# An attention, recurrence and feed-forward block on one core: wider products for the recurrence, modulation moved later, softmax steps of two heads together

## The chip, the cores and the metric

The kernel runs on one core of a Trainium2 chip. The metric is the device time of one execution in microseconds. Of the kernel before there are three timed runs (median 1793.35 us, 1793.25 to 1795.22) and one more execution that was profiled (1793.77 us).

## The reference, cut to what matters

One block is computed for 256 tokens of 2048 features in 32-bit floats (T = 256, D = 2048).

```python
mod = silu(c) @ ada_w + ada_b                 # 6 x 2048: sh1, sc1, g1, sh2, sc2, g2
h = rmsnorm(x) * norm1_g * (1 + sc1) + sh1
z = h @ w_in                                  # q, 6 x kv, gates, lx, ly, ga, gb
o_a = attention(...)                          # compressed, selected and window branch, gated
u = causal_dwconv(lx)                         # 4 taps
r, i = sigmoid(u @ w_a + b_a), sigmoid(u @ w_i + b_i)     # 16 blocks of 128
a = exp(8 * r * log_sigmoid(lam)); b = sqrt(1 - a*a) * i * u
o_b = gelu(ly) * scan(a, b)
merged = sigmoid(ga) * (o_a @ proj_a) + sigmoid(gb) * (o_b @ proj_b)
x = x + g1 * (merged @ w_out)
h = rmsnorm(x) * norm2_g * (1 + sc2) + sh2
x = x + g2 * conv_glu_ffn(h); out = rmsnorm(x) * final_g
```

## The kernel before

**Products in three parts.** Every large product is taken with weights and activations split in a high and a low part. A weight piece of 1 MB is loaded by SyncE's queue into one of four buffers (`stage`, L97 to L100). For each half of it ScalarE copies the high part (L107) and VectorE subtracts it from the weights for the low part (L108), into one of three pairs of `hi` and `lo` buffers (`split`). TensorE adds high by high, high by low and low by high into PSUM. An activation tile `h1[:, kt]` holds its high part in columns 0 to 255 and its low part in columns 256 to 511.

There are three forms of this in the kernel. `dense_tok` (L192) has tokens on the partitions and multiplies 512 columns of weights at a time. `dense_pair` (L114) has features on the partitions: the high weights are multiplied by all 512 columns of the activation tile in one instruction, the low weights by the first 256 columns. Its result lies in two banks of PSUM, one for each of two blocks of 128 features, as two halves of 256 columns that are still to be added. The feed-forward adds them with one VectorE reduction (`reduce`, L225). `dense_pair1` (L172) is used by the recurrence's 16 products (L715, L765): three instructions of 256 columns for each tile (L185, L187, L188), 96 in a call, both blocks of features in a single bank, and nothing to add. One ScalarE instruction of 512 columns takes the result away: a copy into `lx` (L716), or the Gelu (L767). Banks for all these products come from one pool of four (L112).

**Modulation.** `mod` has 96 pieces of 1 MB, one for each 128 of its 12288 columns. The first 32 are needed at the start. The other 64 wait in a list (L513), in the order g1, sc2, sh2, g2. `filler(n)` takes n of them: each loads a piece through the same four buffers and queue as the weights, VectorE multiplies it by the activated condition and sums it (L234), and adds the bias (L235). Before, fillers stand behind the recurrence's products (two behind each of the eight calls that make `lx`, L720, and four in all at L773), behind the merge's projections (L797, 28 in all) and in the first half of the feed-forward (16).

**Order of the work.** A scheduling pass of the compiler orders the instructions of each engine from the program order, with estimated times. `tc.high_priority(200)` moves some earlier. `tc.keep_in_program_order` keeps the instructions so marked in the order of the program: all loads, and the products of `dense_pair`. Engines run their queues in order.

**The stages around the change.** Attention (L632 to L703) handles four heads of one group and 128 tokens in a unit, eight units in all. For each head: scores (L667, L670), the maximum (L676, L677), the exponential with its sum (L679), a reciprocal and the gate (L681 to L683), the scaling (L686), transposes through one PSUM bank (L689) and copies out of it (L691). The eight calls for `lx` are issued among the units. Then come four steps of the recurrence (L725 to L773): convolution, gate products, sigmoids, exponentials and square roots, the scan, and two calls for the Gelu branch each. The merge follows (L781 to L809: gates and projections, `dense_tok`), then the output projection (L839 to L855), whose rows become the input of the feed-forward. Columns 256 and 257 of the tiles `hp` hold the shift sh2 (L823 to L826); the first product of the feed-forward (`dense_shift`, L148 to L150) reads them.

Of the kernel before, what the change touches and what calls it, by code (L numbers as in the profile page):

```python
# [38 lines left out]
def block_kernel(tc, x_t, x_n, gf_row, cols_d, consts_d, ada_w, w_kv0, w_kv, w_v, w_gate, w_q, cmp_w, cmp_w2,  # L39
# [16 lines left out]
    with ExitStack() as es:  # L56
# [57 lines left out]
        def dense_pair(pieces, rhs):  # L114
# [4 lines left out]
            for ip, ap in enumerate(pieces):  # L119
                raw = stage(ap)  # L120
                for half in range(2):
                    hl = split(raw, half * 1024, 1024)
                    done = [0, 0]
                    for w in (0, 0, 1, 0, 1, 0, 1, 1) + (0, 1) * 4 if ip + half == 0 else (0, 1) * 8:
                        f, k = done[w] // 4, done[w] % 4
                        done[w] += 1
                        kt = ip * 8 + half * 4 + k
                        r = rhs(kt)
                        tc.keep_in_program_order(
                            PE.matmul(ps[f][:, 0:256] if w else ps[f], hl[w][:, k * 256 + f * 128:k * 256 + f * 128 + 128],  # L130
                                      r[:, 0:256] if w else r, start=(kt == 0 and not w), stop=(kt == n - 1 and w == 1),
                                      skip_group_check=True))
            return ps

# [37 lines left out]
        def dense_pair1(pieces, rhs):  # L172
            p = bank()
            n = len(pieces) * 8
            for ip, ap in enumerate(pieces):
                raw = stage(ap)
                for half in range(2):
                    hi, lo = split(raw, half * 1024, 1024)
                    for f in range(2):
                        o = p[:, f * 256:f * 256 + 256]  # L180
                        for k in range(4):
                            kt = ip * 8 + half * 4 + k
                            sl = slice(k * 256 + f * 128, k * 256 + f * 128 + 128)
                            r = rhs(kt)
                            PE.matmul(o, hi[:, sl], r[:, 0:256], start=(kt == 0 and f == 0), stop=False,  # L185
                                      skip_group_check=True)
                            PE.matmul(o, hi[:, sl], r[:, 256:512], start=False, stop=False, skip_group_check=True)  # L187
                            PE.matmul(o, lo[:, sl], r[:, 0:256], start=False, stop=(kt == n - 1),  # L188
                                      skip_group_check=True)
            return p  # L190

        def dense_tok(pieces, lhs, late=None):  # L192
# [15 lines left out]
            for ip, ap in enumerate(pieces):  # L208
                raw = stage(ap)
                hold = late is not None and ip >= len(pieces) - 2  # L210
                for half in range(2):
# [6 lines left out]
                    for j in range(2):  # L218
                        products(j, k0, *hl)
            for j in range(2 if held else 0):  # L220
# [411 lines left out]
        def attention(g, t):  # L632
# [31 lines left out]
            nj = 2 * (t + 1)  # L664
            for hh in range(4):
# [9 lines left out]
                sm = tmp.tile([128, 6], F32, tag="sm", bufs=2, name="sm")  # L675
                V.tensor_reduce(sm[:, 0:2], s[:, 0:2 * nk].rearrange("p (b n) -> p b n", b=2), axis=AX, op=ALU.max)  # L676
                V.tensor_scalar(sm[:, 0:2], sm[:, 0:2], -SCALE, None, op0=ALU.mult)  # L677
                for b in range(2):
                    A.activation(p[:, b * nk:b * nk + nk], s[:, b * nk:b * nk + nk], AF.Exp, bias=sm[:, b:b + 1],  # L679
                                 scale=SCALE, accum_out=sm[:, 2 + b:3 + b])  # L680
                V.tensor_scalar(sm[:, 2:4], sm[:, 2:4], 1e-30, None, op0=ALU.max)  # L681
                V.reciprocal(sm[:, 2:4], sm[:, 2:4])
                V.tensor_tensor(sm[:, 4:6], sm[:, 2:4], gates[:, hh, 1:3], op=ALU.mult)  # L683
                for b in range(2):
                    pb = p[:, b * nk:b * nk + nk]
                    V.tensor_scalar(pb, pb, sm[:, 4 + b:5 + b], None, op0=ALU.mult)  # L686
                tp = psx.tile([128, 512], F32, tag="t", bufs=1, name="tp")
                for j in range(nj):
                    PE.transpose(tp[:, j * 128:j * 128 + 128], p[:, j * 128:j * 128 + 128], ident)  # L689
                for n in range(t + 1):  # L690
                    A.activation(pT[n][:, :, hh, :], tp[:, n * 256:n * 256 + 256].rearrange("p (j q) -> p j q", q=128),  # L691
                                 AF.Copy)
# [21 lines left out]
        for pr in range(8):  # L714
            pl = dense_pair1([w_lru[pr, k] for k in range(2)], h1r)  # L715
            A.activation(lx[pr // 2][:, 2 * (pr % 2):2 * (pr % 2) + 2],  # L716
                         pl.rearrange("p (f t) -> p f t", f=2), AF.Copy)
            if units:
                attention(*units.pop(0))
            filler(2)  # L720
# [4 lines left out]
        for bt in range(4):  # L725
# [37 lines left out]
            for h in range(2):  # L763
                pr = bt * 2 + h
                pl = dense_pair1([w_lru[8 + pr, k] for k in range(2)], h1r)  # L765
                gl = u[:, 2 * h:2 * h + 2]
                tbl(A.activation(gl, pl.rearrange("p (f t) -> p f t", f=2), AF.Gelu_apprx_tanh))  # L767
# [5 lines left out]
                filler(2 if pr % 4 == 0 else 0)  # L773
# [7 lines left out]
        for n in range(4):  # L781
            m = []
            for s, rhs in ((0, lambda kt: oA[:, kt]), (1, lambda kt: oB[kt // 2][:, kt % 2])):
# [3 lines left out]
                else:  # L787
                    ps = dense_tok([w_gates[n - 1, s, k] for k in range(4)], h1r)
# [231 lines left out]
```

## Time and profile before

| | |
|---|---|
| median of three timed runs | 1793.35 us |
| profiled execution | 1793.77 us |
| its span, first to last instruction | 1792.0 us |
| TensorE busy | 1771.6 us (99%) |
| VectorE busy | 1350.5 us (75%) |
| ScalarE busy | 881.9 us (49%) |
| mean granted TensorE clock | 0.997 |
| read from HBM | 425.72 MB, 239 GB/s over the span |

The span leaves 1.8 us of the profiled execution outside it. Matmuls overlap in the record, since the next one starts before the last one's modelled end. What a matmul costs in a stream is therefore the distance from one start to the next, not the duration in its row.

### The profile page before, as it was taken

The page shows a single profiled execution, that of the slowest core. Times are in us where ns is not written, and L with a number is a line of the kernel's source. Part 1 is how long each engine was busy: PE and PEld are TensorE (multiplying, and loading weights), DVE is VectorE, ACT ScalarE, POOL GpSimd, SP SyncE. Part 2 cuts the span into 40 slices and gives each one's busy share as a digit, 9 for nine tenths or more (in the row PEclk, how much of TensorE's full clock was granted, in tenths as well). Part 3 has the DMA queues.
Part 4 walks back from the last instruction along what each step waited for, and adds up shares of the span by engine and source line. Part 5 has one row for each costly group of instructions (what it writes and reads, how often), then busy time and mean ns, then how long its engine had stood idle before and what let it go on. Part 6 is the DMA issues. An engine that isn't in the chain of part 4 may idle for free.

```text
span 1792.0 us, 25746 instructions
## 1 busy us (share of the span) xinstructions
PE 1771.6 (99%) x10262; PEld 1545.9 (86%) x10262; DVE 1350.5 (75%) x1976; ACT 881.9 (49%) x1202; POOL 0.2 (0%) x4
## 2 busy tenths in 40 slices
PE   8999999999999999999999999999999999999997
PEld 7999898888999888888888998888888888888886
DVE  7998897998698766767765997888555677766555
ACT  5644464655578444444445644444433444444443
POOL 0000000000000000000000000000000000000000
PEclk9999999999999999999999999999999999999999
DMA  9999864665646867777775566777655555555552
GB/s 350 379 335 355 288 245 161 235 212 203 221 173 227 303 237 290 286 292 281 294 266 195 186 235 235 282 282 282 239 193 200 191 188 188 188 188 188 190 198 106
DMA packets 64200, 429.50 MB, mean 240 GB/s; under 512 B 7088, under 2 KB 7376, under 8 KB 15568
## 3 DMA queue, kind: packets, MB, share of 16 engines
q1 hardware_dynamic: 63792, 427.08, 66.2%
q8 instruction: 80, 1.31, 0.3%
q10 hardware_dynamic: 288, 0.79, 0.1%
q14 instruction: 40, 0.33, 0.1%
HBM read 425.72 MB, written 2.11 MB: 239 GB/s over the span
## 4 chain that ended last, share of the span: by engine, by line
PE 86%; DVE 6%; DMA 4%; issue 2%; ACT 2%; SPq 0%; DVEq 0%; ACTq 0%
PE P L130 26%; PE P L204 12%; PE P L205 12%; PE P L203 12%; PE P L187 3%; PE P L188 3%; PE P L185 3%; DMA raw<-ada_w 2%; DVE lo L108 2%; PE P L464 2%; PE P L466 2%; PE P L465 2%; PE P L149 1%; PE P L148 1%; PE P L150 1%
## 5 line engine op out<-in xcount | busy, mean ns | idle before, releaser
L107 ACT ACTIVATE hi<-raw 128x1024 fp32r<-128x1024 f32 x588 | 622.0, 1060 | 764.5 <-PE P L205 325.5
L108 DVE TENSOR_TENSOR lo<-raw,hi 128x1024 fp32r<-128x1024 f32 x588 | 717.1, 1222 | 370.5 <-ACT hi L107 369.7
L130 PE MATMUL P<-h,hi 128*128 128x512 f32 x1344 | 463.9, 394 | 0.0
L130 PE MATMUL P<-h,lo 128*128 128x256 f32 x1344 | 366.4, 278 | 0.0
L130 PEld LDWEIGHTS P<-h,hi 128*128 128x128 f32 x1344 | 249.1, 188 | 54.9
L130 PEld LDWEIGHTS P<-h,lo 128*128 128x128 f32 x1344 | 252.4, 188 | 4.2
L234 DVE SCALAR_TENSOR_TENSOR raw<-raw,crow 128x2048 f32<-128x2048 f32 x64 | 146.2, 2285 | 3.6 <-DMA raw<-ada_w 3.2
L188 PE MATMUL P<-h,lo 128*128 128x256 f32 x512 | 147.6, 289 | 0.8 <-DVE lo L108 0.8
L187 PE MATMUL P<-h,hi 128*128 128x256 f32 x512 | 146.7, 287 | 0.0
L185 PE MATMUL P<-h,hi 128*128 128x256 f32 x512 | 146.7, 287 | 0.0
L464 PE MATMUL P<-h,hi 128*128 128x256 f32 x384 | 107.9, 285 | 0.3 <-ACT hi L107 0.3
L465 PE MATMUL P<-h,hi 128*128 128x256 f32 x384 | 107.6, 284 | 0.0
L466 PE MATMUL P<-h,lo 128*128 128x256 f32 x384 | 102.2, 284 | 0.0
L188 PEld LDWEIGHTS P<-h,lo 128*128 128x128 f32 x512 | 97.8, 191 | 1.8 <-DVE lo L108 1.4
L187 PEld LDWEIGHTS P<-h,hi 128*128 128x128 f32 x512 | 97.9, 191 | 1.4 <-issue 1.2
L185 PEld LDWEIGHTS P<-h,hi 128*128 128x128 f32 x512 | 97.9, 191 | 1.0 <-issue 0.7
L204 PE MATMUL P<-lo,ua 128*128 128x512 f32 x240 | 93.5, 390 | 0.3 <-DVE lo L108 0.3
L205 PE MATMUL P<-hi,ua 128*128 128x512 f32 x240 | 93.4, 389 | 0.0
L203 PE MATMUL P<-hi,ua 128*128 128x512 f32 x240 | 83.6, 389 | 0.0
L204 PE MATMUL P<-lo,h 128*128 128x512 f32 x192 | 75.5, 393 | 0.0
L464 PEld LDWEIGHTS P<-h,hi 128*128 128x128 f32 x384 | 74.0, 193 | 1.1 <-ACT hi L107 0.5
L205 PE MATMUL P<-hi,h 128*128 128x512 f32 x192 | 74.9, 390 | 0.0
(281 smaller groups left out, 3131.6 us busy)
## 6 DMA issues: line engine op xcount, KB each, us to landing
raw<-ada_w SPq DMA_DIRECT2D x96, 1024.0 KB, 5.0
raw<-w_up SPq DMA_DIRECT2D x96, 1024.0 KB, 4.8
raw<-w_down SPq DMA_DIRECT2D x48, 1024.0 KB, 4.9
raw<-w_lru SPq DMA_DIRECT2D x32, 1024.0 KB, 4.9
raw<-w_proj SPq DMA_DIRECT2D x32, 1024.0 KB, 5.1
raw<-w_gates SPq DMA_DIRECT2D x24, 1024.0 KB, 6.5
raw<-w_out SPq DMA_DIRECT2D x16, 1024.0 KB, 4.9
raw<-w_kv SPq DMA_DIRECT2D x24, 512.0 KB, 6.7
```

Of the source, the lines that this page charges most:

```text
L107: A.activation(hi[:, :n], raw[:, lo_col:lo_col + n], AF.Copy)
L108: V.tensor_tensor(lo[:, :n], raw[:, lo_col:lo_col + n], hi[:, :n].bitcast(F32), op=ALU.subtract)
L130: PE.matmul(ps[f][:, 0:256] if w else ps[f], hl[w][:, k * 256 + f * 128:k * 256 + f * 128 + 128], r[:, 0:256] if w else r, start=(kt == 0 ...
L185: PE.matmul(o, hi[:, sl], r[:, 0:256], start=(kt == 0 and f == 0), stop=False, skip_group_check=True)
L187: PE.matmul(o, hi[:, sl], r[:, 256:512], start=False, stop=False, skip_group_check=True)
L188: PE.matmul(o, lo[:, sl], r[:, 0:256], start=False, stop=(kt == n - 1), skip_group_check=True)
L203: PE.matmul(ps[j], xh, hi[:, w], start=(kt == 0), stop=False, skip_group_check=True)
L204: PE.matmul(ps[j], xh, lo[:, w], start=False, stop=False, skip_group_check=True)
L205: PE.matmul(ps[j], xl, hi[:, w], start=False, stop=(kt == n - 1), skip_group_check=True)
L234: V.scalar_tensor_tensor(raw, raw, 1.0, row, op0=ALU.mult, op1=ALU.mult, accum_out=modc[:, c:c + 1])
L464: PE.matmul(o, hi[:, sl], h1[:, kt, 0:256], start=first and f % 2 == 0, stop=False, skip_group_check=True)
L465: PE.matmul(o, hi[:, sl], h1[:, kt, 256:512], start=False, stop=False, skip_group_check=True)
```

## The change

`dense_pair1` goes; the recurrence's 16 products are made by `dense_pair`, whose new argument leaves the order of its instructions to the scheduling pass. A new helper adds the two halves: ScalarE copies the second half to its destination, and VectorE adds the first half to it. Gelu then reads the sum from SBUF. Of the modulation pieces, 4 instead of 16 stand in the loop over `lx` and none instead of 4 in the recurrence; 36 instead of 28 are in the merge, placed between the weight pieces of one product, and 8 in the output projection. The 16 in the feed-forward stay. The shift columns of `hp` are written behind the output projection. In attention two heads share the steps from the clamp to the gate, and their scaling, transposes and copies follow behind both heads' exponentials.

```diff
-        def dense_pair(pieces, rhs):
+        def dense_pair(pieces, rhs, pinned=True):
 
 
...
-                    for w in (0, 0, 1, 0, 1, 0, 1, 1) + (0, 1) * 4 if ip + half == 0 else (0, 1) * 8:
+                    for w in (0, 0, 1, 0, 1, 0, 1, 1) + (0, 1) * 4 if pinned and ip + half == 0 else (0, 1) * 8:
...
-                        tc.keep_in_program_order(
-                            PE.matmul(ps[f][:, 0:256] if w else ps[f], hl[w][:, k * 256 + f * 128:k * 256 + f * 128 + 128],
-                                      r[:, 0:256] if w else r, start=(kt == 0 and not w), stop=(kt == n - 1 and w == 1),
-                                      skip_group_check=True))
+                        mm = PE.matmul(ps[f][:, 0:256] if w else ps[f],
+                                       hl[w][:, k * 256 + f * 128:k * 256 + f * 128 + 128], r[:, 0:256] if w else r,
+                                       start=(kt == 0 and not w), stop=(kt == n - 1 and w == 1), skip_group_check=True)
+                        if pinned:
+                            tc.keep_in_program_order(mm)
             return ps
+
+        def add_halves(dst, p):
+            A.activation(dst, p[:, 256:512], AF.Copy)
+            with tc.high_priority(200):
+                V.tensor_tensor(dst, p[:, 0:256], dst, op=ALU.add)
 
...
-        def dense_tok(pieces, lhs, late=None):
+        def dense_tok(pieces, lhs, late=None, fills=()):
...
+                if ip in fills:
+                    filler()
...
+            sm = tmp.tile([128, 2, 4, 2], F32, tag="sm", bufs=2, name="sm")
+            heads = []
+
+            def turn_heads(hh):
+                p = heads[hh]
+                for b in range(2):
+                    pb = p[:, b * nk:b * nk + nk]
+                    V.tensor_scalar(pb, pb, sm[:, 1, hh, b:b + 1], None, op0=ALU.mult)
+                tp = psx.tile([128, 512], F32, tag="t", bufs=1, name="tp")
+                for j in range(nj):
+                    PE.transpose(tp[:, j * 128:j * 128 + 128], p[:, j * 128:j * 128 + 128], ident)
+                for n in range(t + 1):
+                    A.activation(pT[n][:, :, hh, :], tp[:, n * 256:n * 256 + 256].rearrange("p (j q) -> p j q", q=128),
+                                 AF.Copy)
+
             for hh in range(4):
...
-                V.tensor_scalar(sm[:, 2:4], sm[:, 2:4], 1e-30, None, op0=ALU.max)
-                V.reciprocal(sm[:, 2:4], sm[:, 2:4])
-                V.tensor_tensor(sm[:, 4:6], sm[:, 2:4], gates[:, hh, 1:3], op=ALU.mult)
...
+                heads.append(p)
+                if hh % 2 == 0:
+                    continue
+                w = sm[:, 1, hh - 1:hh + 1]
+                V.tensor_scalar(w, w, 1e-30, None, op0=ALU.max)
+                V.reciprocal(w, w)
+                V.tensor_tensor(w, w, gates[:, hh - 1:hh + 1, 1:3], op=ALU.mult)
+                turn_heads(hh - 1)
+                turn_heads(hh)
...
         for pr in range(8):
-            pl = dense_pair1([w_lru[pr, k] for k in range(2)], h1r)
-            A.activation(lx[pr // 2][:, 2 * (pr % 2):2 * (pr % 2) + 2],
-                         pl.rearrange("p (f t) -> p f t", f=2), AF.Copy)
+            ps = dense_pair([w_lru[pr, k] for k in range(2)], h1r, False)
+            for f in range(2):
+                add_halves(lx[pr // 2][:, 2 * (pr % 2) + f], ps[f])
             if units:
                 attention(*units.pop(0))
-            filler(2)
+            filler(pr % 2)
...
-                pl = dense_pair1([w_lru[8 + pr, k] for k in range(2)], h1r)
+                ps = dense_pair([w_lru[8 + pr, k] for k in range(2)], h1r, False)
                 gl = u[:, 2 * h:2 * h + 2]
-                tbl(A.activation(gl, pl.rearrange("p (f t) -> p f t", f=2), AF.Gelu_apprx_tanh))
+                for f in range(2):
+                    add_halves(gl[:, f], ps[f])
+                tbl(A.activation(gl, gl, AF.Gelu_apprx_tanh))
...
-                filler(2 if pr % 4 == 0 else 0)
...
-                    ps = dense_tok([w_gates[n - 1, s, k] for k in range(4)], h1r)
+                    ps = dense_tok([w_gates[n - 1, s, k] for k in range(4)], h1r, fills=(1, 3))
...
-                ps = dense_tok([w_proj[n, s, k] for k in range(4)], rhs)
+                ps = dense_tok([w_proj[n, s, k] for k in range(4)], rhs, fills=(0, 1, 3))
...
-                filler(2 if n == 0 else 4)
...
-        filler(max(0, len(fill) - 16))
+        assert len(fill) == 24
...
-        for n in range(8):
-            sh = modc[:, 48 + 2 * n:50 + 2 * n].unsqueeze(2).to_broadcast([128, 2, 2])
-            A.activation(hp[n][:, :, 0, 256:258], sh, AF.Copy)
-            V.tensor_tensor(hp[n][:, :, 1, 256:258], sh, hp[n][:, :, 0, 256:258].bitcast(F32), op=ALU.subtract)
-
...
-            ps = dense_tok([w_out[n, k] for k in range(4)], lambda kt: mg[kt // 2][:, kt % 2])
+            ps = dense_tok([w_out[n, k] for k in range(4)], lambda kt: mg[kt // 2][:, kt % 2],
+                           fills=(0, 1, 3) if n < 2 else (0, 2) if n == 2 else ())
...
+        for n in range(8):
+            sh = modc[:, 48 + 2 * n:50 + 2 * n].unsqueeze(2).to_broadcast([128, 2, 2])
+            A.activation(hp[n][:, :, 0, 256:258], sh, AF.Copy)
+            V.tensor_tensor(hp[n][:, :, 1, 256:258], sh, hp[n][:, :, 0, 256:258].bitcast(F32), op=ALU.subtract)
```

## Rows read from the trace of the kernel before

**Rows 1.** The page's first part: span, busy time and instructions of each engine.
```profile
span 1792.0 us, 25746 instructions
...
PE 1771.6 (99%) x10262; PEld 1545.9 (86%) x10262; DVE 1350.5 (75%) x1976; ACT 881.9 (49%) x1202; POOL 0.2 (0%) x4
```

**Rows 2.** The page's chain that ended last, shares by engine.
```profile
PE 86%; DVE 6%; DMA 4%; issue 2%; ACT 2%; SPq 0%; DVEq 0%; ACTq 0%
```

**Rows 3.** Stretches: length, PE, PEld, DVE, ACT, POOL busy, clock, DMA share, GB/s.
```profile
285.00:585.00 300.00, 298.68 (x2166) 267.68 (x2165) 258.56 (x579) 195.12 (x378) 0.00 (x0) 1.00 0.57 204
480.00:585.00 105.00, 104.18 (x823) 102.18 (x822) 91.07 (x130) 83.07 (x110) 0.00 (x0) 1.00 0.58 209
585.00:985.00 400.00, 400.00 (x1796) 330.63 (x1795) 272.80 (x309) 177.67 (x210) 0.00 (x0) 1.00 0.75 272
660.00:680.00 20.00, 20.00 (x89) 16.33 (x88) 16.26 (x18) 8.08 (x8) 0.00 (x0) 1.00 0.99 384
1060.00:1240.00 180.00, 180.00 (x1038) 157.27 (x1037) 157.98 (x226) 80.09 (x91) 0.00 (x0) 1.00 0.74 265
```

**Rows 4.** TensorE's waits from 285 to 585 us: total, times, longest.
```profile
PEld P L188 <- DVE lo L108: 1.4, 3, 0.9
PE P L188 <- DVE lo L108: 0.8, 2, 0.7
```

**Rows 5.** Timeline of TensorE in a recurrence product: start, duration; 27 starts apart.
```profile
483.74 0.28 PE L188 MATMUL P<-h,lo 128*128 128x256 f32 x1
...
486.98 0.28 PE L188 MATMUL P<-h,lo 128*128 128x256 f32 x1
```

**Rows 6.** The chain in order of time, second half's feed-forward products: start, length.
```profile
1385.19 266.87 PE P L130 x1536
```

**Rows 7.** Timeline of TensorE behind an attention unit's small products.
```profile
427.25 0.36 PE L188 MATMUL P<-h,lo 128*128 128x256 f32 x1
427.45 0.28 PE L185 MATMUL P<-h,hi 128*128 128x256 f32 x1
```

**Rows 8.** Groups by line, ACT and DVE: count, busy us, mean ns, idle before.
```profile
L808 ACT ACTIVATE mg<-turn 128x256 fp32r<-128x256 f32 x16 | 5.2, 377 | 2.8 <-PE turn L806 2.8
L809 DVE TENSOR_TENSOR mg<-turn,mg 128x256 fp32r<-128x256 f32 x16 | 6.0, 415 | 0.0
L716 ACT ACTIVATE lx<-P 128x512 f32<-128x512 f32 x8 | 4.6, 579 | 0.0
L767 ACT ACTIVATE lt<-P 128x512 f32<-128x512 f32 x8 | 4.7, 589 | 0.0
L892 ACT ACTIVATE fgl<-ct 128x512 f32<-128x512 f32 x24 | 15.1, 628 | 5.1 <-DVE ct L889 5.0
L234 DVE SCALAR_TENSOR_TENSOR raw<-raw,crow 128x2048 f32<-128x2048 f32 x64 | 146.2, 2285 | 3.6 <-DMA raw<-ada_w 3.2
L235 DVE TENSOR_TENSOR modc<-modc,cols 128x1 f32<-128x1 f32 x64 | 9.7, 151 | 0.0
L681 DVE TENSOR_SCALAR sm<-sm 128x2 f32<-128x2 f32 x32 | 5.2, 162 | 3.3 <-ACT p L679 3.2
L682 DVE RECIPROCAL sm<-sm 128x2 f32<-128x2 f32 x32 | 5.1, 160 | 0.3
L683 DVE TENSOR_TENSOR sm<-sm,gsig 128x2 f32<-128x2 f32 x32 | 5.0, 155 | 0.3
```

**Rows 9.** Timelines of DVE, PE and ACT around the recurrence's third step.
```profile
543.42 1.22 DVE L758 TENSOR_TENSOR lt<-lt 128x1024 f32<-128x1024 f32 x1
...
546.02 0.28 PE L187 MATMUL P<-h,hi 128*128 128x256 f32 x1
...
551.73 0.60 ACT L767 ACTIVATE lt<-P 128x512 f32<-128x512 f32 x1
```

**Rows 10.** Timelines of PE and ACT where the feed-forward begins.
```profile
983.97 0.28 PE L148 MATMUL P<-hp,hi 128*128 128x258 f32 x1
...
986.75 0.18 ACT L837 ACTIVATION_READ_ACCUMULATOR junk<-res 128x1 f32 x1
```

More of the change, by code (lines that the diff above doesn't have):

```diff
@@ L170, in up @@
             return take
[L172 to L190, printed above, removed]
-        def dense_tok(pieces, lhs, late=None):
+        def dense_tok(pieces, lhs, late=None, fills=()):
             ps = [bank(), bank()]
@@ L674, in attention @@
                     p = tmp.tile([128, 512], F32, tag=("r", "iu", "tt")[hh - 1], bufs=1, name="p")
-                sm = tmp.tile([128, 6], F32, tag="sm", bufs=2, name="sm")
-                V.tensor_reduce(sm[:, 0:2], s[:, 0:2 * nk].rearrange("p (b n) -> p b n", b=2), axis=AX, op=ALU.max)
-                V.tensor_scalar(sm[:, 0:2], sm[:, 0:2], -SCALE, None, op0=ALU.mult)
+                V.tensor_reduce(sm[:, 0, hh], s[:, 0:2 * nk].rearrange("p (b n) -> p b n", b=2), axis=AX, op=ALU.max)
+                V.tensor_scalar(sm[:, 0, hh], sm[:, 0, hh], -SCALE, None, op0=ALU.mult)
                 for b in range(2):
-                    A.activation(p[:, b * nk:b * nk + nk], s[:, b * nk:b * nk + nk], AF.Exp, bias=sm[:, b:b + 1],
-                                 scale=SCALE, accum_out=sm[:, 2 + b:3 + b])
-                V.tensor_scalar(sm[:, 2:4], sm[:, 2:4], 1e-30, None, op0=ALU.max)
-                V.reciprocal(sm[:, 2:4], sm[:, 2:4])
-                V.tensor_tensor(sm[:, 4:6], sm[:, 2:4], gates[:, hh, 1:3], op=ALU.mult)
[L684 to L692, printed above, removed]
+                    A.activation(p[:, b * nk:b * nk + nk], s[:, b * nk:b * nk + nk], AF.Exp, bias=sm[:, 0, hh, b:b + 1],
+                                 scale=SCALE, accum_out=sm[:, 1, hh, b:b + 1])
+                heads.append(p)
[7 more added lines that the diff above has]
+                turn_heads(hh)
             PE.matmul(oT, vcmp[:, g * 128:g * 128 + 128], pcT[0:47], start=True, stop=False,
```

## The prediction

> **What bounds the kernel now.** I read the page's first part first: TensorE is busy for 1771.6 of 1792.0 us [rows 1]. The chain of waits agrees, with 86% on TensorE [rows 2]. A busy record can hide waits, so I then took stretches. From 285 to 585 us, where attention and the recurrence lie, TensorE is idle for 300.00 - 298.68 = 1.3 us; from 585 to 985 us, merge and output projection, it is not idle at all [rows 3]. Its waits in the first stretch are for VectorE's low halves, 1.4 and 0.8 us at most, partly the same time [rows 4]. So the time is the sum of what TensorE issues, and an edit on another engine counts only where it makes TensorE wait. The granted clock is 1.00, the upper level of 2.4 GHz, in every stretch [rows 3].
>
> **The products.** In a recurrence product 27 instructions of 256 columns start within 486.98 - 483.74 = 3.24 us, 0.120 us each [rows 5]; one tile costs three, 0.360 us. The new form already runs in the feed-forward: 1536 instructions, half of them 512 and half 256 columns wide, take 266.87 us [rows 6], so a tile costs 266.87 / 768 = 0.3475 us. Sixteen calls have 32 tiles each: 512 x (0.360 - 0.3475) = **6.4 us less**. TensorE streams the same 768 columns for a tile; only one instruction's fixed part goes. As 256 columns at 2.4 GHz last 0.1067 us, that part is 13.3 ns in rows 5, and 512 x 13.3 ns is 6.8 us, near the same.
>
> The Trainium skill ("TensorE: Matmul & The Clock Gate", Back-to-back issue gap) puts the fixed part of an isolated warm matmul at about 2.5 ns. By it the products would give 512 x 2.5 ns = 1.3 us, an estimate from that page. The trace does not agree, since rows 5 leave 13.3 ns.
>
> The order of the new calls is not fixed as in rows 6; the scheduling pass may group them otherwise. The columns and instructions are the same, so I cost this at nothing; if it placed a low product ahead of its low half, TensorE would wait as in rows 4, some 0.7 us at a time.
>
> **Adding the halves** brings 32 ScalarE copies and 32 VectorE additions of 256 columns from PSUM. The nearest rows have 0.377 and 0.415 us [rows 8]: 12.1 us of ScalarE and 13.3 us of VectorE. Eight copies of 0.579 us go (4.6 us); eight Gelus read SBUF, 0.628 instead of 0.589 us (0.3 us more) [rows 8]. None of this lies on TensorE. It could hold its banks: a call now takes two of the four, not one, so a call's halves must be taken away before the next call but one begins, one call or 32 x 0.3475 = 11.1 us later. In the third step the first call's last product starts about 546.0 us and its Gelu runs at 551.73 us [rows 9], six microseconds later, which would still be in time. The new copy is free earlier: it writes where L758 reads, and L758 is over at 543.42 + 1.22 = 544.6 us, before the products end [rows 9]. Cost: nothing.
>
> **The modulation.** Sixteen pieces leave the stretch 285 to 585 us. Each is 2.285 + 0.151 = 2.44 us of VectorE [rows 8], 39 us in all. With the three small softmax steps done for two heads at once (16 x (0.162 + 0.160 + 0.155) = 7.6 us less [rows 8]), VectorE goes from 258.6 to 258.6 - 39 - 7.6 + 13.3 = 225 us of 300 and ScalarE from 195.1 to 195.1 + 7.8 = 203 us [rows 3]. What TensorE can win there is its whole idle time, 1.3 us, or nothing; I take half, **0.7 us**.
>
> The 16 pieces go to merge and output projection, and their 16 loads of 1.05 MB pass SyncE's queue in front of loads of gate, projection and output weights and of the rows of x. VectorE there goes from 272.8 to 312 us of 400, 78% [rows 3]; in the feed-forward TensorE stays fully busy with VectorE at 157.98 / 180 = 88% [rows 3]. The DMA goes from 272 x 400 = 109 MB to 126 MB, 314 GB/s. From 660 to 680 us 384 GB/s moved while TensorE did not stop [rows 3]. The tightest place is the first output product: four weight pieces, three modulation pieces, the g1 row (1 MB) and half a megabyte of x, 8.5 x 1.05 = 8.9 MB within about 96 x 20 / 89 = 21.6 us, where 384 GB/s need 23.2 us. The four buffers ahead may cover the 1.6 us or not: 0 to 1.6 us.
>
> **The shift columns** now come behind the output projection. Their last modulation piece stands in its third product, so the fourth (21.6 us) hides them if the pass puts them there. If they queue behind the last squares, which end at 986.75 + 0.18 us, TensorE, which begins the feed-forward at 983.97 us [rows 10], waits some 3 us. I take 0.7 us for this and the DMA together, nearer the lower ends, since both have a cover of 20 us or of four buffers.
>
> **Two heads at once** leave TensorE's instructions in attention as they are. Going back from small products to large ones costs 427.45 - 427.25 - 0.12 = 0.08 us [rows 7]. If the transposes of two heads ran together, half of 32 such returns would go, 1.3 us; as they share one PSUM bank, the second head's must wait for copies, so I take nothing. The first head's transposes wait for the second's exponential, with the dense products as cover; the 1.3 us of idle time in the stretch says how well they cover today. A loss is held by the same rows at a few tenths of a microsecond for a head.
>
> **Sum.** 6.4 + 0.7 - 0.7 = 6.4 us less than the profiled execution's 1793.77 us: 1787.4 us. The median of the timed runs stands 0.4 us lower, so I predict **1787.0 us**, 0.35% less. With both upper bounds and no loss it is 6.4 + 1.3 + 1.3 = 9.0 us, 1784.3 us from the median.
>
> **Rivals.**
>
> First, **the recurrence's queues take the place of the wait.** From 480 to 585 us ScalarE is busy for 83.1 us and VectorE for 91.1 us of 105 [rows 3]. The recurrence has only four modulation pieces in its program to lose, and the change adds 16 copies, 16 additions and 0.3 us of Gelu: 6.0 + 6.6 + 0.3 = 12.9 us in two queues that run in order. If each delays a split that TensorE waits for, and it decides as soon as the three pairs of `hi` and `lo` run dry, the kernel takes 1793.35 - 6.4 + 12.9 = **1799.9 us**, slower. For it speaks that both engines would be near 88% of a shorter stretch and that rows 4 show this wait already. Against it: VectorE gets some of its 39 us back just before, so it enters the recurrence ahead, and TensorE idles only 0.8 us there today. Chance 0.08.
>
> Second, **part of the gain is eaten** in that way, or by the shift columns and the DMA (3 + 1.6 us, together 1791.5 us), or by half of the 12.9 us (1793.4 us). Chance 0.12.
>
> Third, **the wider instruction saves nothing**, because time goes by columns: 768 columns at 0.120 / 256 us are 0.360 us again, 1793.35 us. Rows 6 speak against it; it needs the new calls to run worse than the same form in the feed-forward. By the 2.5 ns of the Trainium skill's page named above it would be 1793.35 - 1.3 = 1792.1 us, an estimate and much the same case. Chance 0.04.
>
> Fourth, the waits of the stretch hide more than the idle time shows, and the time falls below 1784.3 us. Chance 0.04. The forecast keeps 0.72.
>
> **Numbers.** A measurement of this kernel can tell about 0.2%, 3.6 us, from no change. Below 1789.8 us lie the forecast and the fourth rival, 0.76; the second and third are within 0.2%, 0.16; the first is slower, 0.08. The range 1784.3 to 1793.4 us holds the forecast and most of the second and third, about 8 in 10.
>
> **What would show it.** Right: the recurrence's calls show 64 instructions, 0.3475 us for a pair, and TensorE's idle time from attention to the recurrence's end stays near 1 us; the same stage is about 6 us shorter and all later stages have their old lengths. Wrong: waits of TensorE for low or high halves of some microseconds in the recurrence, a wait for a bank or for `hp` at the start of the feed-forward, a wait for a modulation piece ahead of VectorE in the output projection, or pairs that cost 0.36 us.

## The result and the profile after

The changed kernel is slower: a median of 1808.6 us (1806.53 to 1809.74, four runs) against 1793.3 us of the kernel before, ratio 1.0083 with a 95% interval of 1.0067 to 1.0099. The profiled execution took 1807.54 us. The page's first part and its chain, by engine:

```profile
span 1805.7 us, 24688 instructions
...
PE 1773.0 (98%) x9750; PEld 1520.2 (84%) x9750; DVE 1359.6 (75%) x1960; ACT 890.6 (49%) x1228; POOL 0.2 (0%) x4
...
PE 76%; DMA 11%; DVE 7%; ACT 2%; issue 2%; DVEq 0%; ACTq 0%
```

The 512 matmuls are gone (10262 to 9750, [rows 1]), yet TensorE's busy time is no shorter and the span is 13.7 us longer. The chain has 11% on DMA, where it had 4% [rows 2]. The same columns as in [rows 3], for the stretches that answer to those:

```profile
285.00:593.00 308.00, 296.96 (x1631) 239.84 (x1630) 228.70 (x508) 201.04 (x399) 0.00 (x0) 0.98 0.41 145
485.00:593.00 108.00, 100.74 (x529) 84.48 (x528) 86.61 (x131) 86.98 (x123) 0.00 (x0) 0.97 0.49 172
593.00:998.00 405.00, 402.81 (x1802) 331.70 (x1802) 309.76 (x361) 179.08 (x215) 0.00 (x0) 1.00 0.82 309
1073.00:1253.00 180.00, 180.00 (x1038) 157.41 (x1037) 157.85 (x226) 80.34 (x91) 0.00 (x0) 1.00 0.72 264
```

From the first attention product to the merge's first, the kernel before took 297.9 us (287.2 to 585.1) and the changed one 306.7 (286.1 to 592.8): 8.8 us more, with TensorE idle for 308.00 - 296.96 = 11.0 us where it had been idle for 1.3 [rows 3]. The merge takes 313.9 us in place of 308.0, 5.9 more; the output projection 91.0 and 90.9, and all behind it 808.0 in both. The start is 1.1 us shorter. Part of the merge's 5.9 us is the recurrence's: in the changed kernel the last of its products still run from 593.3 to 595.6 us, behind the merge's first. Counted with them, attention and recurrence are 11.1 us longer and the merge 3.6. VectorE's and ScalarE's loads came out as worked out: 228.7 and 201.0 us in the first stretch (predicted 225 and 203), VectorE 309.8 us behind it (predicted 312). What was wrong is who waits.

TensorE's longest waits from 465 to 593 us:

```profile
PE P L129 <- DVE lo L108: 6.5, 4, 3.0
PE lru_r L745 <- ACT p L682: 1.7, 1, 1.7
PE P L129 <- DVE lx L139: 1.1, 1, 1.1
```

In two stretches there the clock falls as well, to its lower level of 1.2 GHz for some microseconds; in the kernel before it is 1.00 in every 20 us from 280 to 1240 us:

```profile
470.00:480.00 10.00, 6.75 (x27) 5.16 (x28) 5.86 (x19) 4.76 (x15) 0.00 (x0) 0.83 0.11 44
520.00:530.00 10.00, 6.88 (x26) 5.41 (x25) 10.00 (x21) 9.46 (x13) 0.00 (x0) 0.72 0.42 159
```

**The first of them** is where the eight calls for `lx` are done and attention is not. The timeline of TensorE, then the additions of the halves into `lx` on VectorE:

```profile
465.83 0.36 PE L129 MATMUL P<-h,lo 128*128 128x256 f32 x1
466.03 1.03 PE L745 MATMUL lru_r<-lt,raw 128*128 128x256 f32 x4
467.32 1.98 PE L697 MATMUL oT<-pT,vN 128*128 128x512 f32 x4 [0.27 <-ACT pT L666]
469.14 0.60 PE L648 MATMUL tpc<-cols,cmpb 128*47 128x128 f32 x4
471.44 1.13 PE L745 MATMUL lru_r<-lt,raw 128*128 128x256 f32 x4 [1.70 <-ACT p L682]
472.41 0.64 PE L664 MATMUL tp<-cols,p 128*128 128x128 f32 x4
473.80 0.66 PE L664 MATMUL tp<-cols,p 128*128 128x128 f32 x4 [0.75 <-ACT pT L666]
474.39 0.49 PE L693 MATMUL oT<-pcT,cmpb 47*128 47x512 f32 x1
475.94 0.50 PE L129 MATMUL P<-h,hi 128*128 128x512 f32 x1 [1.06 <-DVE lx L139]
...
433.09 0.42 DVE L139 TENSOR_TENSOR lx<-P,lx 128x256 f32<-128x256 f32 x1
475.46 0.42 DVE L139 TENSOR_TENSOR lx<-P,lx 128x256 f32<-128x256 f32 x1 [1.42 <-ACT lx L137]
```

Between 433 and 475 us no half is added, though the seventh and the eighth call finish at 451 and 466 us. Both write `lx[3]`, which takes the buffer C7 of `cmpb`, and attention's last unit reads that at 474.39 us (L693). So two calls hold all four banks, and no large product can start before 475.94 us. Before, the last L693 ended at 461.5 us, and two waiting calls would have held two banks.

**The products themselves** became cheaper, as predicted. Three starts of a recurrence product:

```profile
483.62 0.39 PE L129 MATMUL P<-h,hi 128*128 128x512 f32 x1
483.85 0.28 PE L129 MATMUL P<-h,lo 128*128 128x256 f32 x1
483.96 0.39 PE L129 MATMUL P<-h,hi 128*128 128x512 f32 x1
```

A pair takes 483.96 - 483.62 = 0.34 us, against 0.360 us for three [rows 5].

**In the merge** the modulation pieces are waited for. The group of their multiplication over the whole run, to be held against [rows 8], and the waits of VectorE and of SyncE's queue from 593 to 998 us:

```profile
L223 DVE SCALAR_TENSOR_TENSOR raw<-raw,crow 128x2048 f32<-128x2048 f32 x64 | 146.5, 2290 | 59.3 <-DMA raw<-ada_w 59.3
...
DVE raw L223 <- DMA raw<-ada_w: 54.6, 34, 3.4
...
SPq L53 <- DVE raw L223: 206.4, 43, 7.2
```

VectorE stands idle 59.3 us in front of pieces that have not landed, 3.6 us before. The queue in turn waits 206.4 us for these multiplications to give a buffer free; in the kernel before this was 29.8 us in the merge and output projection. Its waits for the buffers of the splits (L108) fell at the same time, from 253.7 to 124.6 us, so not all of the 206.4 us is new. TensorE waits 2.0 us for low halves in this stretch, where it did not wait before.

### The profile page after: what moved, and what is told of

It is laid out like the page before. It is cut to its first block, busy times and chain, and to the rows that moved or that the text cites. A ratio compares the mean times of both kernels' runs of the same rounds, so it can differ in the third digit from the quotient of the medians.

```text
span 1805.7 us, 24688 instructions
## 1 busy us (share of the span) xinstructions
PE 1773.0 (98%) x9750; PEld 1520.2 (84%) x9750; DVE 1359.6 (75%) x1960; ACT 890.6 (49%) x1228; POOL 0.2 (0%) x4
## 4 chain that ended last, share of the span: by engine, by line
PE 76%; DMA 11%; DVE 7%; ACT 2%; issue 2%; DVEq 0%; ACTq 0%
PE P L129 34%; DMA raw<-ada_w 11%; PE P L191 7%; PE P L192 7%; PE P L190 6%; DVE raw L223 3%; PE P L453 2%; PE P L455 2%; PE P L454 2%; DVE lo L108 2%; PE P L447 1%; PE P L448 1%; PE P L446 1%; PE P L155 1%; PE P L154 1%
## 5 line engine op out<-in xcount | busy, mean ns | idle before, releaser
L108 DVE TENSOR_TENSOR lo<-raw,hi 128x1024 fp32r<-128x1024 f32 x588 | 715.9, 1222 | 308.9 <-ACT hi L107 308.2
L129 PE MATMUL P<-h,hi 128*128 128x512 f32 x1856 | 650.1, 398 | 1.7 <-DVE lx L139 1.1
L129 PEld LDWEIGHTS P<-h,hi 128*128 128x128 f32 x1856 | 346.7, 189 | 77.3 <-DVE lx L139 1.4
L129 PEld LDWEIGHTS P<-h,lo 128*128 128x128 f32 x1856 | 351.6, 189 | 15.5 <-DVE lo L108 9.4
L223 DVE SCALAR_TENSOR_TENSOR raw<-raw,crow 128x2048 f32<-128x2048 f32 x64 | 146.5, 2290 | 59.3 <-DMA raw<-ada_w 59.3
L453 PE MATMUL P<-h,hi 128*128 128x256 f32 x384 | 108.0, 286 | 0.0
L454 PE MATMUL P<-h,hi 128*128 128x256 f32 x384 | 107.7, 285 | 0.0
L192 PE MATMUL P<-hi,h 128*128 128x512 f32 x192 | 75.0, 390 | 0.0
L453 PEld LDWEIGHTS P<-h,hi 128*128 128x128 f32 x384 | 74.1, 193 | 0.5 <-issue 0.2
L454 PEld LDWEIGHTS P<-h,hi 128*128 128x128 f32 x384 | 74.1, 193 | 0.0
L312 DVE SCALAR_TENSOR_TENSOR raw<-raw,crow 128x2048 f32<-128x2048 f32 x31 | 70.7, 2284 | 1.8 <-DMA raw<-ada_w 1.4
L455 PEld LDWEIGHTS P<-h,lo 128*128 128x128 f32 x384 | 70.7, 192 | 0.3 <-issue 0.2
L190 PE MATMUL P<-hi,h 128*128 128x512 f32 x192 | 68.2, 394 | 0.0
L155 PE MATMUL P<-hp,hi 128*128 128x258 f32 x192 | 54.0, 284 | 0.0
L191 PEld LDWEIGHTS P<-lo,ua 128*128 128x128 f32 x240 | 45.1, 188 | 10.1 <-DVE lo L108 0.8
```

The lines of the kernel that those rows point to most:

```text
L108: V.tensor_tensor(lo[:, :n], raw[:, lo_col:lo_col + n], hi[:, :n].bitcast(F32), op=ALU.subtract)
L129: mm = PE.matmul(ps[f][:, 0:256] if w else ps[f], hl[w][:, k * 256 + f * 128:k * 256 + f * 128 + 128], r[:, 0:256] if w else r, start=(kt ...
L155: PE.matmul(o, hi[:, sl], r[:, 1], start=False, stop=False, skip_group_check=True)
L190: PE.matmul(ps[j], xh, hi[:, w], start=(kt == 0), stop=False, skip_group_check=True)
L191: PE.matmul(ps[j], xh, lo[:, w], start=False, stop=False, skip_group_check=True)
L192: PE.matmul(ps[j], xl, hi[:, w], start=False, stop=(kt == n - 1), skip_group_check=True)
```

## The experiments

The theories: **B**, two calls hold all four banks. **S**, the scheduling pass puts more dense work ahead of attention's end, so that the recurrence's chain starts late. **Q**, the added copies and additions delay the low halves in the recurrence. **H**, the steps of two heads lengthen attention. **M**, the moved modulation makes VectorE wait for loads. Every ratio is to the kernel before on the same chip, with its 95% interval.

### The three parts, alone and in pairs

Each kernel has one or two of the diff's three parts whole: products (`dense_pair`, `add_halves`), modulation (the `fills`, the counts and the place of the shift columns), heads (`turn_heads`).

> The kernel before with the wide products and the added halves alone; modulation and attention as before. Theory B (banks: the last two calls for lx hold all four banks until the buffer of lx[3] is given up by the last attention unit, so TensorE has no dense work there): about 1793.3 - 6.4 + 6 to 9 for an empty stretch near the end of attention = 1793 to 1796 us. Theory H (steps of two heads make attention outlast the calls for lx): 1787 us, no empty stretch. Theory M (the moved modulation makes VectorE wait for loads): 1787 us.

> The kernel before with the modulation pieces moved alone. Theory M: merge and output projection 4 to 6 us longer, VectorE idle some 50 us in front of modulation pieces, and the recurrence's end a little late: 1797 to 1800 us. Theories B and H: 1793 us or a little less, since VectorE is relieved in attention.

> The kernel before with the steps of two heads at once alone. Theory H: attention's last unit ends some 10 to 18 us later than 476 us and TensorE has empty stretches there: 1798 to 1803 us. Theories B and M: 1793 us within 2 us, TensorE without empty stretches.

> The changed kernel with attention's steps one head at a time again. Theory H: the empty stretches from 466 to 480 us go, about 8 us less than the changed kernel: 1799 to 1801 us. Theory B: they stay, as two calls still hold the four banks until the last unit: 1806 to 1809 us. Theory M says nothing of this stretch and expects the 4 to 6 us of the merge in it as in the changed kernel.

> The changed kernel with the modulation where it was before: wide products and the steps of two heads. Theory M: merge and output projection as long as before, the changed kernel's loss there (5 to 6 us) gone: 1801 to 1803 us. If the moved modulation also helped attention by taking VectorE's load away, it gives some of that back: 1804 to 1807 us.

> The changed kernel with the narrow products: modulation moved and the steps of two heads. If the parts add up, 6.6 + 2.5 us above before: 1802 to 1803 us. If the steps of two heads cost much only together with the wide products (late end of attention, banks held), as the runs with both suggest, they cost nothing here: 1800 to 1801 us.

| parts | median us | before us | ratio |
|---|---|---|---|
| products | 1803.25 | 1794.59 | 1.0051 (1.0039 to 1.0063) |
| modulation | 1801.31 | 1794.59 | 1.0037 (1.0024 to 1.0050) |
| heads | 1796.73 | 1794.59 | 1.0014 (1.0005 to 1.0022) |
| products, modulation | 1805.81 | 1794.59 | 1.0067 (1.0054 to 1.0081) |
| products, heads | 1809.47 | 1793.27 | 1.0089 (1.0076 to 1.0102) |
| modulation, heads | 1804.97 | 1794.31 | 1.0052 (1.0037 to 1.0066) |
| all three | 1808.6 | 1793.3 | 1.0083 (1.0067 to 1.0099) |

Every part costs time by itself. The products, worth 6.4 us of TensorE, cost 8.7, and the 1793 to 1796 us that B expected of them was missed by 7 us: B is not their whole loss. H in its strong form falls: the heads alone cost some 2 us, not 5 to 10. With modulation they add up (1.0037 and 1.0014 make 1.0051, measured 1.0052); with the products they cost more, 1.0089 instead of 1.0065, but beside products and modulation only 1.0083 - 1.0067 = 0.16% again. The expectation for the run without modulation missed: taking the modulation back did not make the changed kernel faster. So the modulation's loss does not add to the other two: with them attention ends later still when the pieces are back (501.5 us for the last subtraction into `oA`, 494.9 in the changed kernel, 476.1 before). That the pieces' load on VectorE does this was not tested by itself.

With the products alone the empty stretch is there, and ScalarE's wait names the cause, the copy of the halves behind attention's L693 (here L679). From 465 to 480 us:

```profile
ACT lx L137 <- PE oT L679: 2.3, 1, 2.3
```

### The banks

```diff
-            ps = dense_pair([w_lru[pr, k] for k in range(2)], h1r, False)
+            if pr < 6:
+                ps = dense_pair([w_lru[pr, k] for k in range(2)], h1r, False)
...
+            else:
+                pl = dense_pair1([w_lru[pr, k] for k in range(2)], h1r)
```

This is on the kernel with the products alone; `lx6_wide` has the Gelu calls narrow as well.

> The wide products alone, as in the run with them alone, but the last two calls for lx in the narrow form (one bank each). Theory B (banks): no empty stretch of TensorE between 465 and 485 us and no fall of the clock there, some 8 us less than with all calls wide: 1793 to 1796 us, what is left being waits for low halves from 510 to 590 us. If the empty stretch had another cause (attention simply late), it stays: 1801 to 1804 us.

> Only the first six calls for lx wide, the last two and the eight Gelu calls narrow as before. Theory B: no empty stretch; theory Q (the additions and copies in the recurrence delay the low halves): waits for low halves in the recurrence as in the kernel before, about 1 us; the gain of six calls, 6 x 32 x 0.0125 = 2.4 us, is left: 1790 to 1793 us, 1 to 3 us less than the kernel before and 2 to 5 us less than with the Gelu calls wide too. Without Q it is no faster than with the Gelu calls wide.

Measured: 1800.5 us, 1.0032 (1.0020 to 1.0045), and 1794.37 us, 1.0002 (0.9993 to 1.0011). The empty stretch is gone, as B says; the same columns as above:

```profile
465.00:485.00 20.00, 20.00 (x127) 17.76 (x126) 14.64 (x26) 12.23 (x20) 0.00 (x0) 1.00 0.56 193
485.00:590.00 105.00, 96.56 (x497) 80.25 (x496) 85.36 (x132) 82.63 (x119) 0.00 (x0) 0.97 0.49 179
```

But only about 3 of the 8 us came back, fewer than expected: TensorE now idles 105.00 - 96.56 = 8.4 us in the recurrence. The banks put the idle time where it was seen first; they are not the whole cause. Making the eight Gelu calls narrow again took another 5 to 6 us away (1.0032 to 1.0002), though it gives up 8 x 32 x 0.0125 = 3.2 us of TensorE. What is left, six wide calls, gains nothing and misses its 1790 to 1793 us.

The three ratios, 1.0051, 1.0032 and 1.0002, divide the products' loss once. To each step is added the 0.0125 us a tile that the narrow form gives up. The last two calls for `lx` lost 3.4 + 0.8 = 4.2 us by being wide, the eight Gelu calls 5.4 + 3.2 = 8.6 us, and the other six calls 0.4 + 2.4 = 2.8 us. These are estimates, each uncertain by 2 to 3 us, and they hold for this order of steps. The Gelu calls carry the largest share.

### The order of the dense work

Counted in the traces, the columns of split products that TensorE streams between attention's first and last product are 8.85 calls' worth (24576 columns each) in the kernel before, 9.95 with the products alone, 10.28 in the changed kernel, 9.10 with the heads alone. The last subtraction into `oA` ends at 476.1, 493.3, 494.9 and 480.7 us. Before, and then in the changed kernel, it reads:

```profile
475.42 0.69 DVE L702 TENSOR_TENSOR oA<-oT,oA 128x512 fp32r<-128x512 f32 x1 [0.51 <-ACT oA L701]
...
494.16 0.69 DVE L702 TENSOR_TENSOR oA<-oT,oA 128x512 fp32r<-128x512 f32 x1 [2.09 <-ACT oA L701]
```

To test whether that matters, the last two calls were queued behind attention's output products of the seventh and the last unit (`HELD` names the call and the unit it waits for):

```diff
+            with ExitStack() as behind:
+                if pr in HELD:
+                    behind.enter_context(tc.issue_after(marks[HELD[pr]].ins))
-            ps = dense_pair([w_lru[pr, k] for k in range(2)], h1r, False)
+                ps = dense_pair([w_lru[pr, k] for k in range(2)], h1r, False)
```

> All sixteen products wide and nothing else changed, but the seventh and eighth call for lx are queued on TensorE behind the seventh and the last attention unit's first output product. Theory S (the scheduling pass puts more dense work ahead of attention's end, the recurrence's chain starts late, and TensorE runs out of work behind it): attention's last product comes near 475 us instead of 492, the first recurrence step is some 12 us earlier, no empty stretch, and 6 to 10 us less than with the wide products alone: 1793 to 1797 us. If the recurrence's waits come only from the added copies and additions (theory Q), the empty stretch goes, but the waits from 510 to 590 us stay: 1799 to 1802 us.

> The eight calls for lx wide and the last two held as in the run above, the Gelu calls narrow as before. Theory S: 8 x 32 x 0.0125 = 3.2 us less than the kernel before, 1790 to 1792 us, and less than with six wide calls and no hold. Theory Q alone: the same as with six wide calls, 1793 to 1795 us, as the hold does nothing for the recurrence.

> A candidate: all products wide, only the last call for lx held behind the last attention unit's first output product (so that TensorE has dense work ahead of it), and the Gelu's halves added by VectorE's reduction. Theory S: about as early an end of attention as in the first run with a hold, without its gap near 432 us: 1790 to 1795 us. If only the longer hold helps: 1797 us or more.

`held_wide`: 1797.13 us, 1.0016 (1.0007 to 1.0025), 8.92 calls' worth, `oA` done at 481.6 us. The hold gives back 0.35%, some 6 us of the 15 that the products fell short of their worth (8.7 + 6.4). It does not tell S from B, since the two calls no longer hold all four banks either; by the steps above, B alone is worth about 4 of the 6. And `lx6_wide` has `oA` done at 488.4 us, 12.3 later than the kernel before, at the time of the kernel before. So a late end of attention by itself costs at most some 3 us there; that S carries most of the loss is not shown. The hold makes a spot of its own, since the seventh call is now kept while TensorE waits for attention's transposes, and the clock falls there:

```profile
425.00:435.00 10.00, 8.02 (x46) 5.99 (x45) 9.46 (x31) 6.15 (x20) 0.00 (x0) 0.99 0.84 306
435.00:445.00 10.00, 10.00 (x32) 6.04 (x31) 6.58 (x27) 3.44 (x14) 0.00 (x0) 0.66 0.43 160
```

`held_lx_wide` missed its 1790 to 1792 us: 1796.37 us, 1.0020 (1.0011 to 1.0028), with runs from 1793.24 to 1802.06. With the two calls held and no added work at the Gelus it should have gained, by S, and it did not. Its profiled execution is one of the shortest, so its rows say little of the median. The candidate `held_last_reduce` missed too: 1800.43 us, 1.0032 (1.0020 to 1.0044); with one call held, `oA` was late again (487.4 us). Why the pass orders more dense work ahead in the wide form was not settled.

### The added work in the recurrence

`gelu_reduce` is `lx6_gelu_wide` with VectorE's reduction in place of copy and addition. `spare_adds` is the kernel before with the added work alone:

```diff
+                for f in range(2):
+                    spare = tmp.tile([128, 256], F32, tag="xp", bufs=2, name="spare")
+                    A.activation(spare, pl[:, f * 256:f * 256 + 256], AF.Copy)
+                    with tc.high_priority(200):
+                        V.tensor_tensor(spare, pl[:, f * 256:f * 256 + 256], spare, op=ALU.add)
                 tbl(A.activation(gl, pl.rearrange("p (f t) -> p f t", f=2), AF.Gelu_apprx_tanh))
```

> Six wide calls for lx and wide Gelu calls, as in the run of that name, but the Gelu's halves are added by one VectorE reduction for each bank, as the feed-forward does, in place of a ScalarE copy and a VectorE addition: 16 ScalarE copies go (6 us), VectorE has 16 x (0.69 - 0.42) = 4 us more. If ScalarE's queue is what delays the chain, 2 to 4 us less: 1796 to 1798 us. If VectorE's is, 2 to 4 us more: 1802 to 1805 us. If neither (theory S: the late start), within 2 us of it.

> The kernel before with spare work in the recurrence alone: ahead of each of the eight Gelus, two ScalarE copies and two VectorE additions of 256 columns into a spare tile, as many as the change puts there; the products stay narrow and take one bank a call, and the spare results are not used. Theory Q (the added copies and additions by themselves delay the low halves): 3 to 6 us more than before and waits of TensorE for low halves from 510 to 590 us. Theory S (the recurrence starts late, behind more dense work and a later end of attention, and the banks): within 1 us of the kernel before.

`gelu_reduce`: 1797.89 us, 1.0022 (1.0013 to 1.0030), some 2 us less than with copies, towards the smaller load of ScalarE, though the two intervals overlap. `spare_adds`: 1799.41 us beside 1794.31, 1.0029 (1.0018 to 1.0041). So Q holds without the wide products: 32 small instructions that no product needs cost 5.1 us. Part of this may be the test's own, since the spare tile has two buffers: ScalarE's copies wait 6.1 us, four times, for an earlier addition to leave one, and the copies of the changed kernel have no such wait. Its stretch from 480 to 590 us, one around the longest wait, and TensorE's waits from 480 to 592 us:

```profile
480.00:590.00 110.00, 106.08 (x831) 103.54 (x830) 91.85 (x137) 86.04 (x123) 0.00 (x0) 1.00 0.57 207
550.00:562.00 12.00, 9.48 (x77) 9.08 (x76) 12.00 (x24) 10.78 (x15) 0.00 (x0) 1.00 0.47 173
...
PE P L188 <- DVE lo L108: 3.2, 2, 1.9
PE P L185 <- ACT hi L107: 0.6, 1, 0.6
```

VectorE's share from 480 to 590 us is 91.85 / 110 = 84%, no more than before (91.07 / 105 = 87%, [rows 3]). It is the spots that decide: from 550 to 562 us VectorE has no free moment and the low half waits its turn. The last of the four exponentials of the recurrence (L756) starts 92.9 us behind the first; in the kernel before it is 81.0 us.

### The modulation

The three variants are on the kernel with the modulation alone. `modulation_bursts` has all pieces of a product behind it, `modulation_early` loads each one weight piece sooner, and `modulation_12_36` keeps 12 in the loop over `lx`, puts 36 behind the merge's products and none in the output projection. Their edits, in this order (the last line is in the loop over `lx`):

```diff
-                if ip in fills:
-                    filler()
...
+            filler(len(fills))
             return ps
...
+                piece = filler_load() if ip in fills else None
                 raw = stage(ap)
...
+                if piece:
+                    filler_sum(*piece)
...
+            filler(1 + pr % 2)
```

> The modulation moved alone, with the same number of pieces in each product, but all of them behind the product as in the kernel before, none between its weight pieces. Theory M1 (a piece between two weight pieces is multiplied before it has landed, and its buffer holds up the next weights): VectorE's idle time in front of the pieces falls from 68 to under 20 us, the merge and output projection are within 2 us of before, 1794 to 1797 us. Theory M2 (more pieces there are simply too much for the DMA): 1799 to 1803 us as with them between.

> The modulation moved alone, in the same places, but each piece is loaded ahead of the weight piece that it follows and multiplied behind it. Theory M1: it has landed by then, VectorE's idle time in front of the pieces falls under 20 us and the merge is 3 to 5 us shorter than with the move alone: 1795 to 1798 us. Theory M2: no change, 1799 to 1803 us. If the piece holds its buffer for longer and that costs the weights as much, it is no better either, with the idle time gone.

> The modulation moved in part: 12 pieces stay in the loop over lx, none in the recurrence, 36 in the merge, all behind their products, none in the output projection; the shift columns behind the output projection as in the change. Theory M1 (it is the pieces between weight pieces and those in the output projection that cost): merge and output projection as long as before, within 2 us of the kernel before: 1792 to 1796 us. Theory M2 (the DMA has no room for more than 28 in the merge): 4 us more or worse, 1797 to 1801 us.

Measured: 1800.72 us, 1.0032 (1.0020 to 1.0043); 1801.75 us, 1.0041 (1.0028 to 1.0054); 1796.41 us, 1.0013 (1.0004 to 1.0021). The first two missed M1's ranges, and the third is 0.4 us above its own. In the bursts VectorE's idle time in front of the pieces fell from 68.0 to 18.0 us and the merge takes 305.6 us, 6 less than with the move alone, but the output projection grew to 97.1 us (91.4), so the sum is no better and the expected 1794 to 1797 us was missed. Some 2 us of both changes is work that crossed the border: ten instructions of the merge run behind the output projection's first product. Loading sooner left 57.6 us of that idle time and gained nothing; that a load ahead also takes its buffer earlier may be why, but it was not tested. With 36 pieces behind the merge's products and none behind the output's, the waits from 587 to 986 us are far smaller again:

```profile
SPq L53 <- DVE raw L236: 68.9, 28, 4.1
...
DVE raw L236 <- DMA raw<-ada_w: 11.3, 7, 2.2
```

Merge and output projection together take 398.8 us then, 398.9 in the kernel before and 403.1 with the move alone. So the merge has room for 36 pieces; their place between weight pieces and those in the output projection cost 4 us there, with some 2 us of the loss left.

The rest lies ahead of the merge, where the expectation had only a recurrence that ends "a little late". With the move alone the stretch from the first attention product to the merge's first takes 302.2 us, 4.3 more than before, though VectorE has fewer pieces there and the first exponential of the recurrence comes at 485.1 us, earlier than before. TensorE waits 2.4 us once for a high half, and the granted clock is 0.94 from 510 to 520 us and 0.89 from 520 to 530 us. With 12 pieces kept it is 300.1 us. Why was not tested.

## Why the prediction was wrong

The sign was wrong, and 1808.6 us is beyond the slowest rival's 1799.9.

The step that failed is that the work around TensorE was put at nothing: drains, added instructions and waiting loads made it wait, 11.0 us from 285 to 593 us where about 1 us was forecast.

- **The products' term was right.** A pair costs 0.34 to 0.35 us in the recurrence too at the upper clock, and 512 instructions are gone. The 2.5 ns fixed part of the page "TensorE: Matmul & The Clock Gate" (Back-to-back issue gap) in the Trainium skill does not fit here: the row of 1536 instructions, again 266.87 us for 24 calls in the changed kernel, leaves 266.87 / 1536 - 0.160 = 0.014 us beyond its 384 columns on average at 2.4 GHz. The page gives the 2.5 ns for an isolated matmul.
- **"It could hold its banks ... Cost: nothing"** failed. I looked at the Gelu's drains and not at those for `lx`, whose last buffer attention still reads. The rule I wrote, that a call's halves must leave before the next call but one, was right; at 451 and 466 us they could not. B is shown by the drains at 475 us and by the run with two narrow calls, which closes the stretch; it is worth about 4 us.
- **"The scheduling pass may group them otherwise ... I cost this at nothing"** failed too. The same work in a cheaper form was put further ahead of attention's end, by 1.1 calls' worth with the products alone. In the changed kernel `oA` was done 18.8 us later, and the first exponential of the recurrence came at 504.0 instead of 489.8 us. Holding two calls back returned 0.35% of the time, the banks' share with it; six wide calls, with `oA` done at 488.4 us, lost little more than their own gain, some 3 us.
- **"None of this lies on TensorE"**, of copies and additions, failed as the first rival says, and it is the dearest step. The rival's price was 12.9 us as a bound; the wide Gelu calls with their added work lost about 8.6 us against their worth, the spare instructions 5.1 us. I gave it 0.08 because VectorE was to enter the recurrence ahead. It could not: the second gate product of the recurrence's first step (L747) takes attention's PSUM banks, and it ran at 493.3 us, before at 479.3.
- **The modulation** was to gain 0.7 us by VectorE's relief and lose at most 1.6 us to the DMA. Alone it costs 6.7 us. The sums of load and bytes were right (VectorE 309.8 of 405 us, 309 GB/s). The step that failed reads a share of 78% as cover. Multiplications that waited for their loads, 54.6 us in all, stood ahead of low halves in VectorE's queue, and the chain that ended last has 11% on loads of modulation weights, before 2%. That the buffers they held also delayed the next weights fits the queue's waits but was not separated. About half of the loss lies ahead of the merge and stays open.
- **Two heads at once** were put at nothing, with a possible loss of a few tenths of a microsecond a head. Alone they cost 0.14%, about 2 us; beside the wide products 0.38%, beside products and modulation 0.16%. No run says why.
- **The shift columns** cost nothing: all from the feed-forward's first product on takes 808.0 us in both kernels, and the output projection 91.0 and 90.9 us.
- What I called TensorE's idle time was taken as a measure of how well its neighbours cover it. Idle time of 1.3 us does not say whether they have room or are just in time; the runs showed the second.

Not settled: why the pass orders more dense work ahead, and how the products' loss of some 15 us (8.7 measured, 6.4 expected as a gain) divides exactly. The runs give about 4 us to the banks of the last two `lx` calls, 5 to 9 us to the wide Gelu calls and their added work, and some 3 us to the rest, the order among it.

## What to carry to other kernels

A change that shortens the bounding engine's work pays only while the other chain, here attention and the four recurrence steps behind it, stays hidden: look when that chain starts and ends before and after, not at the engines' shares. Where a result takes more banks, follow every drain to the buffer that it writes and to that buffer's last reader. Do not put an instruction that waits for a load between the halves that feed TensorE in one engine's queue: here the same 36 pieces cost the merge nothing behind its products.

## What the runs showed of the hardware

The granted clock fell to its lower level within a stretch in which TensorE still had work, 0.83 from 470 to 480 us and 0.72 from 520 to 530 us, each with idle spots of some 3 us in all, and pairs there took 0.64 us from one 512-column start to the next instead of 0.34. Not every idle spot does this: behind a wait of 2.23 us the clock stayed at 1.00. The second spot, and then the one that left the clock alone:

```profile
525.35 0.58 PE L129 MATMUL P<-h,lo 128*128 128x256 f32 x1 [3.03 <-DVE lo L108]
525.73 0.63 PE L129 MATMUL P<-h,hi 128*128 128x512 f32 x1
526.15 0.42 PE L129 MATMUL P<-h,lo 128*128 128x256 f32 x1
526.37 0.63 PE L129 MATMUL P<-h,hi 128*128 128x512 f32 x1
...
556.24 0.39 PE L129 MATMUL P<-h,lo 128*128 128x256 f32 x1 [2.23 <-DVE lo L108]
552.00:562.00 10.00, 7.77 (x45) 6.27 (x43) 10.00 (x18) 9.63 (x12) 0.00 (x0) 1.00 0.53 197
```

So an idle spot can cost more than its own length: from 525.73 to 531.36 us nine pairs took 5.63 us, 2.5 more than nine of 0.3475. I had not expected either that 32 instructions of 0.4 us, on engines at 84 and 78% of a stretch, would cost some 5 us.
